# Layer A's product of probabilities with v of pairs 0 to 4 placed inside the next pair's key projection, ahead of its evacuation

## The chip, the core and the metric

The kernel runs on one core of one Trainium2 chip. The metric is the time of one execution on the device in microseconds (us). A core has a matrix engine (TensorE, PE in the profile, with its weight loads as PEld), a vector engine (VectorE, DVE), a scalar engine (ScalarE, ACT), a general engine (GpSimd, POOL) and an engine that here only starts transfers (SyncE, SP). Each works through its own list of instructions in order. Matmuls write to PSUM, of which this kernel holds four banks for projections (`ps_acc`) and four for everything else (`ps_side`).

## The reference, cut to what matters

Two layers over 512 tokens of width 1024, with 16 heads of 64. Layer A (the one that is touched) is attention in three dilation groups, merged by their denominators; layer B is attention over a two-dimensional neighbourhood. Each layer takes an RMS norm, one input projection (q, k, v of all groups and a gate), the mixer, a product with the gate, one output projection and a residual sum.

```python
def mixer_a(hn, w_in, w_out, q_gain, k_gain, t5_bias):
    proj = hn @ w_in
    qkv = proj[..., :n_qkv].reshape(b, s, N_DIL_GROUPS, 3, N_HEADS, HEAD_DIM)
    gate = proj[..., n_qkv:]
    for g, (window, dilation) in enumerate(DILATED_PAIRS):   # (128, 1), (512, 4), (2048, 16)
        q = rms_norm(qkv[:, :, g, 0], q_gain[g])
        k = rms_norm(qkv[:, :, g, 1], k_gain[g])
        v = qkv[:, :, g, 2]
        o, lse = dilated_group_attention(q, k, v, ...)       # softmax(q k * scale + bias) v
...
    alpha = jax.nn.softmax(jnp.stack(lses), axis=0)
    y = jnp.sum(alpha[..., None] * jnp.stack(outs), axis=0)
    y = y.reshape(b, s, BRANCH_WIDTH).astype(hn.dtype) * jax.nn.silu(gate)
    return y @ w_out
```

## The kernel before

**Tiling.** The 16 heads are handled as eight pairs (`hc` 0 to 7), 128 columns of q, k and v in each dilation group. The projections keep float32 accuracy by splitting each operand into a high and a low part and adding three products (`mm3`, L232), so one step over 128 rows of the contraction is three matmuls of 512 columns for each 128x512 result.

**The main stream (`main_a`, L628).** For each pair it runs four projections on TensorE: the keys of groups 1 and 2 with their v (`rawk`, 8 k-steps of 4 tiles of 3 matmuls, 96 in all), the three queries and the key of group 0 (`rawq`, 96), v of group 0 (`v0_a`, 24) and the gate (`gate_a`, 24). The weights come by DMA (`wraw`, L191) and are split into high and low part on ScalarE (L127) and on VectorE or GpSimd (L133), with four buffers of each. At the last k-step of `rawk` and `rawq` each of the four accumulators is evacuated by ScalarE (L530); then follow squares on GpSimd (L308), sums on VectorE (L311), the inverse root and the scaling (L330).

**The side stream (`side`, L1289).** One pair later, attention is worked in between the projections. For a pair p it runs, in this order:

- `move_q` (L684): the queries and keys, transposed on VectorE (L566), are written to a scratch buffer in DRAM (qd, L691) and read back (qt, L697) with rows and columns exchanged; `land` (L704) scales them on ScalarE (L758) once the next pair's key projection is stamped.
- `attn_a` (L886), in two halves u: scores (the tiles named log), softmax on VectorE (L929, L940) and ScalarE (L951, L802), and the transposing of the probabilities on VectorE (L865). `turner.send` (L867) writes them to a scratch buffer in DRAM (td, L874) and sets four reads back to come due (pt, L878).
- `weigh` (L962): the product of the probabilities with v, 52 small matmuls into two banks named o. `whole` (L778) adds the two banks (ScalarE copy L781, VectorE sum L782), and `put_y` (L804) multiplies by the gate (L822) and splits the result for the output projection (ScalarE L827, GpSimd L828). `attn_a` doesn't run this itself: it appends it to the list `pending`, from which a later point of the side stream takes it.

**What sets the order.** TensorE runs in the order in which the program is written down (`manual_schedule`, L55). That order is made by a planner, `run` (L1032): `clock[0]` adds up a cost for each matmul (512 columns by 1/2.4 ns, 213 ns, for those of the projections; L222), and after every three matmuls of the main stream `pump` (L1036) looks whether the side stream is due. A side step that yields a number is due that many ns later; one that yields nothing, 1200 ns later in layer A; one that yields `"wait", key, delay` is due `delay` ns after the planner's clock at which `key` was stamped:

```python
                if wait[0] is not None:
                    key, delay = wait[0]
                    if key not in stamp:
                        assert until is None, (key, until)
                        return
                    due[0] = max(due[0], stamp[key] + delay)
                    wait[0] = None
                if until is None and clock[0] < due[0]:
                    return
```

`stamp["rawk", hc]` is set when the key projection of pair hc is written down (`normed`, L556), `stamp["gate", hc]` when its gate projection is (`gated`, L785). `later_on` (L246) sets a job, most of them DMAs, to a planner's time, and `tick` (L251) runs what has come due. The order on the other engines comes from a scheduler, except that an instruction marked `keep_in_program_order` stays behind the one written before it on its engine. The writes of qd and td and the reads of qt and pt, all on SyncE, are marked so; the weight loads of layer A are not.

**The period.** With R as the planner's time of `stamp["rawk", hc]`, in planner-us: the weighing of pair hc - 2 is written down at R + 1.92 and costs 2.88; scores u = 0 of pair hc - 1 are due at R + 5.2 and u = 1 at R + 16.8 (12.5 for pair 0), each at a cost of 1.60; the probabilities of u = 1 are sent to td 9.0 after these scores, and their four reads come due 6.0, 6.5, 7.0 and 7.5 after the sending. `move_q` of pair hc is due 8.0 after the end of its query projection, the write of qd 0.6 later and the reads of qt 6.5 later. The gate of pair hc follows, and then the key projection of pair hc + 1.

Of the kernel before, what the change touches and what calls it, by code (L numbers as in the profile page):

```python
# [51 lines left out]
def tile_hybrid_encoder(  # L52
# [193 lines left out]
    def later_on(delay, job):  # L246

        timers.append((clock[0] + delay, job))
        timers.sort(key=lambda t: t[0])
# [494 lines left out]
    def v_a(hc):  # L744

        if hc < NHC - 1:
            return
        yield "wait", ("vt", hc), 2500
        vt = st.pop(("vt", hc))
        tp = bank("tp")  # L750
        for i in range(4):
            transpose(tp[:, i * P : (i + 1) * P], vt[:, i * P : (i + 1) * P])
        nc.scalar.copy(v0[hc % 2], tp.rearrange("p (i c) -> p i c", i=4))
        stamp["v", hc] = 0
        yield
# [48 lines left out]
    def put_y(hc, o, permuted, last):  # L804

        gt, rest = st.pop(("gate", hc))
        for _ in rest:
            pass
        if last and permuted:
            for c in range(4):  # L810
                q = slice(P * c, P * c + P)
                of = lambda t: t.rearrange("p (r c) -> p r c", r=8)[:, :, 16 * c : 16 * c + 16]
                nc.vector.tensor_mul(of(gt), of(gt), of(o))
                src = gt.rearrange("p (t a c) -> p c a t", t=4, a=2)[:, 16 * c : 16 * c + 16]
                h, l = (t[:, hc, q].rearrange("p (c a t) -> p c a t", c=16, a=2) for t in (st["y_h"], st["y_l"]))
                nc.scalar.copy(h, src)
                nc.vector.tensor_sub(l, src, h.bitcast(F32))
            return
        h, l, src = st["y_h"][:, hc, :], st["y_l"][:, hc, :], gt
        if permuted:  # L820

            tc.keep_in_program_order(nc.vector.tensor_mul(gt, gt, o))  # L822
            src = gt.rearrange("p (t a c) -> p c a t", t=4, a=2)
            h, l = (t.rearrange("p (c a t) -> p c a t", t=4, a=2) for t in (h, l))
        else:
            nc.vector.tensor_mul(gt, gt, o)
        nc.scalar.copy(h, src)  # L827
        (nc.vector if last else nc.gpsimd).tensor_sub(l, src, h.bitcast(F32))  # L828
        stamp["ya" if permuted else "yb", hc, "y"] = 0
# [56 lines left out]
    def attn_a(hc):  # L886
# [7 lines left out]
        def scores(u):  # L894

            tiles = []
            for t in (2 * u, 2 * u + 1):
                cs, n = (64, 192) if t == 0 else (0, 192) if t == 3 else (0, 256)
                tiles.append((t, [bank("log") for _ in range(2)], cs, n))
            for t, lgs, cs, n in tiles:  # L900
                ks = slice(P * t + cs, P * t + cs + n)
                parts = [(0, j, slice(cs, cs + n), k0[:, ks]) for j in range(4)] + [
                    (1 + g, j, slice(256 + P * g, 384 + P * g), qt[:, :, 4 + g, 32 * j : 32 * j + 32])
                    for g in range(2)
                    for j in range(4)
                ]
                for g, j, cols, keys in parts:
                    for hd in range(2):
                        hs = slice(64 * hd, 64 * hd + 64)
                        matmul(  # L910
                            lgs[hd][32 * j : 32 * j + 32, cols],
                            qt[hs, t, g, 32 * j : 32 * j + 32],
                            keys[hs],
                            share=2,
                            start=(g == 0),
                            stop=(g == 2),
                        )
            return [
                (hd, t, softmax(hd, t, lgs[hd], cs, n)) for t, lgs, cs, n in tiles for hd in range(2)
            ]  # L920
# [34 lines left out]
        def turn_p(hd, t, pr):  # L955
            tp = bank("tp")
            for i in range(4):
                transpose(tp[:, i * P : (i + 1) * P], pr[:, i * P : (i + 1) * P])
            dst = sb(pts[0], at(t, 0, hd, 0), [[128, 2], [32, 2], [512, 4], [1, 32]])
            nc.vector.tensor_copy(dst, tp.rearrange("p (g i a r) -> p g i a r", g=2, i=2, a=4))  # L960
# [31 lines left out]
        if hc < NHC - 1:  # L992
            for u in range(2):
                if moved(hc):
                    if pending and u == 0:
                        pending.pop(0)()
                        yield
                    yield "wait", ("rawk", hc + 1), 5200 if u == 0 else 16800 if hc else 12500
                else:
                    yield 6500 if u == 0 else 7000  # L1000
                turned = turner(512)
                turners.append(turned)
                for hd, t, pr in scores(u):
                    turned.put(pr, 512, 256 * hd + 64 * (t % 2), 128)
                send = partial(turned.send, pq[:, 2048 * u : 2048 * u + 2048], *((6000, 500) if u else (8500, 1200)))
                later_on(7000 + 2000 * u, send)
                if pending and u == 0:
                    yield 5000
                    pending.pop(0)()
            pending.append(lambda: put_y(hc, weigh(), True, False))  # L1010
        else:
            for u in range(2):
                if u == 0:
                    yield "wait", ("gate", hc), 500
                yield 600
                held = scores(u)
                yield 3200
                if pending:
                    yield "wait", ("gate", hc - 1), 16800
                    pending.pop(0)()  # L1020
                    yield
                for args in held:
                    turn_p(*args)
                    yield
            yield from v_a(hc)
            stamp["ya", "turned"] = 0
            put_y(hc, weigh(), True, True)
            yield

    pending = []  # L1030
# [258 lines left out]
    def side():  # L1289
        for k in range(KT):  # L1290
            norm(0, k, x_all[:, k, :])
            if k:
                square_a(k - 1)
            stamp["na", k] = 0
            if k == 4:
                gains()
            yield 1000
        square_a(KT - 1)
        for k in range(1, KT):
            yield 1300  # L1300
            nc.vector.tensor_add(x_all[:, 0, :], x_all[:, 0, :], x_all[:, k, :])
        yield 1500
        row_scale(row_sums(x_all[:, 0, :]))
        y = big.tile([P, 2 * KT * S], F32R, tag="y", name="y").rearrange("p (n k t) -> p n k t", n=2, k=KT)
        st["y_h"], st["y_l"] = y[:, 0], y[:, 1]
        yield 2500
        bias_lines()
        later_on(21000, lambda: st.__setitem__(("e", 0), bias_a(0)))
        yield 2500
        scales_a()  # L1310
        first_out()
        stamp["rs", "a"] = 0
        for hc in range(NHC):
            if hc < NHC - 1:
                yield from k_a(hc)
                yield from chain(q_a(hc), v_a(hc))
                if moved(hc):
                    yield from st.pop(("land", hc))
                yield from attn_a(hc)
                if hc == 1:  # L1320
                    bias_rows()
            else:
                gap[0] = cycle((500, 500, 700))
                yield from chain(q_a(hc), k_a(hc))
                yield from attn_a(hc)
        yield from residual(xg, 0)
        yield from residual(xg, 4)
        stamp["ya", KT - 1, "y"] = 0
        yield "wait", ("x", KT - 1), 800
        for f in range(KT):  # L1330
            square_b(f)
            yield 600
        yield 4500
        row_scale(row_sums(st.pop("ssq")))
        stamp["rs", "b"] = 0
        yield 5000
        nc.scalar.mul(rs_half, spread(), 0.5)
        stamp["rs", "all"] = 0
        for job, hc, delay in B_PLAN:
            yield "wait", ("b", "start"), delay  # L1340
            if job == "scores":
                yield from side_b(hc)
                continue
            yield "wait", ("back", hc), 3500
            if hc == NHC - 2:
                stamp["yb", "turned"] = 0
            pending.pop(0)()
            yield
            if hc >= NHC - 2:
                yield from residual(xm_d, 4 * (hc % 2))  # L1350

    run(main(), side())


# [98 lines left out]
```

## Time and profile before

| | us |
|---|---|
| median of 3 runs | 815.9 (813.92 to 817.93) |
| the profiled execution, its own time | 817.6 |
| its span, first to last instruction | 815.8 |
| mean granted clock of TensorE, share of full speed | 1.000 |
| VectorE busy | 532.0 |
| ScalarE busy | 434.6 |
| GpSimd busy | 246.9 |

The engines work at the same time, so busy times are not added. Layer A's eight pairs fill the first 540 us or so of the span; its output projection and layer B follow. In the rows below, a line such as L226 is the line of the kernel at which an instruction is issued (all matmuls pass through one helper, so they are told apart by the tile that they write: acc for projections, log for scores, o for the weighing, tp for transposes). "out<-in" names the tile that is written and those read; SPq is SyncE's queue of transfers, and "to landing" is the time from the issue of a DMA until its data are there.

### The profile page before, as it was taken

To read this page: it belongs to the slowest core of one execution; us is meant where nothing else is said; L and a number is where in the kernel's file an instruction comes from. 1 tells how busy PE (TensorE), PEld (TensorE's weight loads), DVE (VectorE), ACT (ScalarE), POOL (GpSimd) and SP (SyncE) were. 2 spreads that over 40 slices of the span, in tenths; PEclk is the share of its full clock that TensorE was granted. 3 is DMA by queue.
4 is the path that set the end of the run, shared out by engine and by line. 5 is a ranking of instruction groups with operands and counts; after the bars stand their busy time and mean duration, and the time that the engine had idled before them with its cause. 6 is when DMAs were issued, how large, how long until landed. Compare 5 with 4: busy or idle time off the path is not lost.

```text
span 815.8 us, 16172 instructions
## 1 busy us (share of the span) xinstructions
PE 808.5 (99%) x5972; PEld 662.2 (81%) x5972; DVE 532.0 (65%) x1364; ACT 434.6 (53%) x913; POOL 246.9 (30%) x400
## 2 busy tenths in 40 slices
PE   9999999999999999999999999999999999999998
PEld 7888888788888888888788888888888887778787
DVE  7466575665576576477476765538656989897824
ACT  7352752752752752662662564536337665757821
POOL 2262441542441441441432342111221315040100
PEclk9999999999999999999999999999999999999999
DMA  7367879779879779968858555157353887698664
GB/s 261 106 207 232 224 216 266 208 200 301 210 210 316 195 220 292 240 186 277 226 164 233 179 160 135 41 193 250 119 164 129 245 230 213 200 268 244 174 213 155
DMA packets 86478, 169.33 MB, mean 208 GB/s; under 512 B 7504, under 2 KB 45520, under 8 KB 86400
## 3 DMA queue, kind: packets, MB, share of 16 engines
q1 hardware_dynamic: 86256, 168.04, 70.0%
q8 instruction: 47, 0.77, 0.4%
q10 hardware_dynamic: 144, 0.26, 0.1%
q14 instruction: 31, 0.25, 0.1%
HBM read 126.21 MB, written 48.22 MB: 214 GB/s over the span
## 4 chain that ended last, share of the span: by engine, by line
PE 92%; DVE 3%; ACT 3%; DMA 1%; issue 1%; SPq 0%; DVEq 0%
PE acc L226 82%; PE log L226 5%; PE o L226 4%; ACT p L1222 1%; PE tp L230 1%; ACT p L1228 1%; DVE wl L133 1%; DMA eb<-eb_d 1%; DMA x_all<-in_xt 0%; DVE rawq L330 0%; DVE rawq L716 0%; PE pa L226 0%; DVE tr L865 0%; ACT wh L127 0%; PE pk L226 0%
## 5 line engine op out<-in xcount | busy, mean ns | idle before, releaser
L226 PE MATMUL acc<-wh,hn_h 128*128 128x512 f32 x704 | 278.8, 397 | 1.2 <-ACT hn_h L419 0.8
L226 PE MATMUL acc<-wl,hn_h 128*128 128x512 f32 x704 | 274.4, 391 | 0.0
L226 PE MATMUL acc<-wh,hn_l 128*128 128x512 f32 x704 | 274.3, 390 | 0.0
L127 ACT CAST wh<-wraw 128x512 fp32r<-128x512 f32 (+1 forms) x240 | 146.2, 613 | 227.0 <-PE acc L226 204.1
L133 DVE TENSOR_TENSOR wl<-wraw,wh 128x512 fp32r<-128x512 f32 (+1 forms) x169 | 121.7, 721 | 132.8 <-ACT wh L127 131.7
L133 POOL TENSOR_TENSOR wl<-wraw,wh 128x512 fp32r<-128x512 f32 (+1 forms) x72 | 94.3, 1310 | 237.8 <-ACT wh L127 228.4
L226 PEld LDWEIGHTS acc<-wh,hn_h 128*128 128x128 f32 x704 | 132.6, 189 | 32.9 <-issue 3.3
L226 PEld LDWEIGHTS acc<-wh,hn_l 128*128 128x128 f32 x704 | 132.7, 189 | 28.0
L226 PEld LDWEIGHTS acc<-wl,hn_h 128*128 128x128 f32 x704 | 132.8, 189 | 26.3
L308 POOL TENSOR_TENSOR sq<-rawq 128x256 f32<-128x256 f32 (+1 forms) x80 | 63.4, 806 | 87.1 <-ACT rawq L530 76.3
L226 PE MATMUL acc<-y,wh 128*128 128x512 f32 (+1 forms) x272 | 81.5, 383 | 0.0
L226 PE MATMUL acc<-hn_h,wh 128*128 128x512 f32 x192 | 75.5, 393 | 0.0
L226 PE MATMUL acc<-hn_l,wh 128*128 128x512 f32 x192 | 74.7, 389 | 0.0
L226 PE MATMUL acc<-hn_h,wl 128*128 128x512 f32 x192 | 74.7, 389 | 0.0
L865 DVE STREAM_TRANSPOSE tr<-p 128x512 f32<-128x512 f32 (+1 forms) x88 | 58.2, 677 | 19.8 <-ACT p L1228 9.0
L311 DVE TENSOR_REDUCE ss<-sq 128x4 f32<-128x256 f32 (+1 forms) x96 | 48.3, 505 | 34.3 <-POOL sq L308 27.4
L951 ACT ACTIVATE p<-p,mn 128x512 f32<-128x512 f32 (+1 forms) x64 | 44.9, 702 | 25.5 <-DVE mn L940 25.5
L226 PEld LDWEIGHTS acc<-y,wh 128*128 128x128 f32 x272 | 48.8, 188 | 9.4 <-issue 0.9
L330 DVE TENSOR_TENSOR rawq<-rawq,rs 128x256 f32<-128x256 f32 (+1 forms) x96 | 51.2, 593 | 5.3 <-POOL rs L119 4.9
L226 PE MATMUL acc<-y,wl 128*128 128x512 f32 (+1 forms) x136 | 51.3, 377 | 0.0
L530 ACT ACTIVATE rawq<-acc,rs_n 128x512 f32<-128x512 f32 (+1 forms) x76 | 44.2, 611 | 0.7 <-PE acc L226 0.2
L802 ACT ACTIVATE p<-p,mn 128x512 f32<-128x512 f32 (+1 forms) x64 | 43.4, 699 | 0.8 <-DVE mn L801 0.7
(142 smaller groups left out, 950.2 us busy)
## 6 DMA issues: line engine op xcount, KB each, us to landing
wraw<-in_w SPq DMA_DIRECT2D x111, 512.0 KB, 5.3
td<-tr SPq DMA_DIRECT2D x14, 1024.0 KB, 6.2
pt<-td SPq DMA_DIRECT2D x56, 256.0 KB, 6.4
qd<-rawq SPq DMA_DIRECT2D x6, 1536.0 KB, 6.6
qt<-qd SPq DMA_DIRECT2D x24, 384.0 KB, 7.4
td<-tr SPq DMA_DIRECT2D x8, 896.0 KB, 4.8
pt<-td SPq DMA_DIRECT2D x32, 224.0 KB, 6.5
v0x<-in_w SPq DMA_DIRECT2D x8, 512.0 KB, 6.0
```

Of the source, the lines that this page charges most:

```text
L127: nc.scalar.copy(h, raw)
L133: eng.tensor_sub(l, raw, h.bitcast(F32))
L226: nc.tensor.matmul(o, l, r, **kw)
L230: nc.tensor.transpose(o, i, ident)
L308: nc.gpsimd.tensor_mul(sq.rearrange("p (f a r) -> p a f r", a=4, r=32), v, v)
L311: nc.vector.tensor_reduce(ss[:, i * ns : (i + 1) * ns], sq.rearrange("p (a b) -> p a b", b=64), axis=AX.X, op=ALU.add)
L330: m = nc.vector.tensor_mul(v, v, by)
L530: nc.scalar.activation(dst, src, AF.Copy, scale=rs_n[:, i : i + 1])
L802: nc.scalar.activation(pr, pr, AF.Copy, scale=mn[:, 3:4])
L865: nc.vector.transpose(dst, src[:, :n].rearrange(order, b=4, k=32, **({"g": 2} if apart else {})))
L951: nc.scalar.activation(row, row, AF.Exp, bias=mn[:, 1:2], scale=-1.0, accum_out=mn[:, 2:3])
L1222: nc.scalar.activation(pr[:, o : o + n], pr[:, o : o + n], AF.Exp, bias=mn[:, 0:1], scale=-1.0, accum_out=mn[:, 2:3])
```

## The change

The weighing of pair hc - 1 is no longer taken from `pending` at the head of `attn_a(hc)`, which runs after the key projection of pair hc + 1 is stamped, but ahead of `land`, 9.0 planner-us after the gate of pair hc is stamped, while that key projection is being written down. `moved(hc)` holds for pairs 0 to 5, and `pending` is empty for pair 0, so the weighings of pairs 0 to 4 are concerned. Those of pairs 5 to 7 stay where they are. What the weighing computes is the same.

```diff
@@ -992,9 +992,6 @@
         if hc < NHC - 1:
             for u in range(2):
                 if moved(hc):
-                    if pending and u == 0:
-                        pending.pop(0)()
-                        yield
                     yield "wait", ("rawk", hc + 1), 5200 if u == 0 else 16800 if hc else 12500
                 else:
                     yield 6500 if u == 0 else 7000
@@ -1315,6 +1312,10 @@
                 yield from k_a(hc)
                 yield from chain(q_a(hc), v_a(hc))
                 if moved(hc):
+                    if pending:
+                        yield "wait", ("gate", hc), 9000
+                        pending.pop(0)()
+                        yield
                     yield from st.pop(("land", hc))
                 yield from attn_a(hc)
                 if hc == 1:
```

## The prediction

> **What bounds the kernel now.** I read the page first, then the table of waits for TensorE, then the chain of waits in order of time, and last SyncE's timeline for the transfers that the moved product needs.
>
> ```profile
> span 815.8 us, 16172 instructions
> PE 808.5 (99%) x5972; PEld 662.2 (81%) x5972; DVE 532.0 (65%) x1364; ACT 434.6 (53%) x913; POOL 246.9 (30%) x400
> ```
>
> TensorE is busy 808.5 of 815.8 us and runs its instructions in the order written. No matmul is added or removed, so the change can act only through the time in which TensorE stands still.
>
> ```profile
> PE log L226 <- issue: 1.8, 2, 1.1
> ```
>
> That row, from the waits, is all the standing still that layer A's attention has: two waits of the score matmuls (log), 1.8 us together, never more than 1.1. The chain shows where they are, and how the weighing (o) lies between the projections (acc). Columns: start, us, what, and matmuls with some of their weight loads counted in.
>
> ```profile
> 102.28 44.46 PE acc L226 x195
> 146.75 3.11 PE o L226 x104
> 149.85 1.59 PE acc L226 x6
> 151.44 1.53 PE log L226 x68
> 152.98 0.78 issue
> 153.76 0.66 PE log L226 x28
> 154.41 10.43 PE acc L226 x45
> 164.84 1.92 PE log L226 x90
> 166.76 43.06 PE acc L226 x189
> 209.82 3.11 PE o L226 x104
> ...
> 226.88 1.96 PE log L226 x90
> ...
> 288.89 1.93 PE log L226 x90
> ...
> 338.58 2.29 PE log L226 x82
> ...
> 351.30 1.92 PE log L226 x87
> ...
> 400.98 1.57 PE log L226 x75
> 402.55 1.05 issue
> 403.61 0.63 PE log L226 x21
> ```
>
> Each o block is one of the five that move. It follows 9 matmuls after a key projection's end: 6 more follow it, then comes the first half of the next pair's scores, then 45, then the second half (164.84). From there to the next o are 189 matmuls in 43.06 us, 0.228 us each: 36 left of the query projection, 24 of v, 24 of the gate, 96 of the next key projection, and 9. So o starts on the instant that its order gives; nothing of it is waited for.
>
> **Step 1: where the weighing goes.** It becomes due 9.0 planner-us after the stamp of the gate. The planner counts 0.2133 for a matmul and looks every three of them: 15 times 0.64 is the first sum that reaches 9.0, so 45 matmuls of the key projection stand ahead and 51 behind. Counted from the second half of the scores: these are due 16.8 planner-us after the key stamp, and the weighing (2.88 planner-us) no longer lies in that stretch, so 72 and not 60 matmuls precede them, and 24 of the query projection are left. Then come 24 of v, 24 of the gate and 45: 117 matmuls by 0.228 is 26.7 us, and with the scores' own 1.92 the weighing is reached 28.6 us after their start. For pair 0 the stretch ahead is old, and 195 less 60 matmuls give 102.28 + 30.8 = 133.1.
>
> **Step 2: what it needs by then.** All rows of the turned probabilities (pt), whose last quarter comes by DMA from a scratch buffer (td) through SyncE's one queue. SyncE's timeline, last column the count:
>
> ```profile
> 123.00 0.43 SPq L878 DMA_DIRECT2D pt<-td  x1
> ...
> 187.44 1.27 SPq L878 DMA_DIRECT2D pt<-td  x3
> 192.77 0.38 SPq L691 DMA_DIRECT2D qd<-rawq  x1
> 193.21 0.50 SPq L878 DMA_DIRECT2D pt<-td  x1
> ...
> 254.62 0.50 SPq L878 DMA_DIRECT2D pt<-td  x1
> ...
> 316.61 1.56 SPq L878 DMA_DIRECT2D pt<-td  x2
> ...
> 379.04 1.56 SPq L878 DMA_DIRECT2D pt<-td  x2
> ```
>
> The DMA view of the moments of these last issues (pairs 0, 1, 2, 3) gives the median time to landing; pair 4's row is the same as pair 3's:
>
> ```profile
> pt<-td SPq DMA_DIRECT2D x1, 256.0 KB, 10.3
> pt<-td SPq DMA_DIRECT2D x1, 256.0 KB, 7.5
> pt<-td SPq DMA_DIRECT2D x1, 256.0 KB, 7.9
> pt<-td SPq DMA_DIRECT2D x2, 256.0 KB, 7.7
> ```
>
> Landings are therefore 133.3 (pair 0), 200.7, 262.5, 324.3 and 386.7; for pairs 1 to 4 that is 35.9, 35.6, 35.4 and 35.4 us after the start of their second scores (164.84, 226.88, 288.89, 351.30), on average 35.6. Before, o comes 45 us after that start and has 9 us to spare. At 28.6 it is 7.0 us early. For pair 0 it is 0.2 early (133.1 against 133.3).
>
> **Step 3: how the landing itself moves.** The last read stands in the queue behind the write of the turned queries (qd), and this waits for VectorE's transposes of rawq, at the end of a chain that starts with the query projection's evacuation:
>
> ```profile
> 171.50 1.32 ACT L802 ACTIVATE p<-p,mn 128x512 f32<-128x512 f32 x2
> 173.76 2.40 ACT L530 ACTIVATE rawq<-acc,rs_n 128x512 f32<-128x512 f32 x4
> 190.38 2.36 DVE L566 STREAM_TRANSPOSE rawq<-rawq 128x1024 f32<-128x1024 f32 x2
> ```
>
> By the change the query projection ends 12 matmuls, 2.7 us, sooner after the scores. If the whole chain follows, qd leaves 2.7 us sooner and the wait is 4.3. But ScalarE works on the scores' softmax until 172.8, 8.0 us after their start, and only then evacuates; if that stays first, nothing is gained. On the other side, the planner's due times now fall the other way round: qd's write is due at 32.6 planner-us after the key stamp, the four reads at 34.2 to 35.7, where before three of them (two, for pairs 3 and 4) came due ahead of qd. All four reads, pinned in program order, now stand behind it: 0 to 0.9 us later (two more issues of 0.43). So the wait is 4.3 to 7.9 per pair; I take the middle of the shift and most of the issues, **6.3 us**. While o waits, the 51 matmuls and the key evacuation behind it wait too, and everything that they feed; nothing hides it, since TensorE is the bound. It returns at pairs 1 to 4: each period's chain is tied to its own key projection, so a wait doesn't spare the next one. 4 times 6.3 is 25.2, and pair 0's 0.2 makes 25.4.
>
> **Step 4: what goes, and what is free.** The two waits of 0.78 and 1.05 us in the scores come right behind a weighing: I take 1.8 off. All of the excess over a plain block of 1.92 us (2.97, 3.25 and 2.29 at 151.44, 400.98 and 338.58) would be 2.8; nothing would be 0.
>
> ```profile
> q8 instruction: 47, 0.77, 0.4%
> ```
>
> I read these 47 transfers as the supply of TensorE's instructions (5972 matmuls and as many weight loads); o and log are its densest stretches, so late instructions are my reading of the two waits. [...]
>
> The product's followers move with it. The copy and the sum are short, and go where ScalarE waits for TensorE 2 us ahead of each weight cast:
>
> ```profile
> L781 ACT COPY ow<-o x8: 566/587/588, 149.9 to 537.1; 128x512 f32<-128x512 f32 x8
> L782 DVE TENSOR_TENSOR ow<-ow,o x8: 679/687/689, 150.5 to 537.7; 128x512 f32<-128x512 f32 x8
> 202.38 0.62 ACT L127 CAST wh<-wraw 128x512 fp32r<-128x512 f32 x1 [2.05 <-PE acc L226]
> ```
>
> I cost them at nothing: the split weights are held four deep (four k-steps of 12 matmuls, 2.7 us each). If that cover were gone, they would cost their 1.3 us per pair. They carry no DMA. The weighing itself takes 3.11 us in either place.
>
> **The sum.** 25.4 less 1.8 is +23.6 us on the profiled execution, 817.6 us (span 815.8 and 1.8 around it). The median of the three runs, 815.9, is 1.7 lower: **839.5 us**, slower by 2.9%. Its own range: 4 times 4.3 less 2.8 is +14.4 (830), 4 times 7.9 with nothing saved is +31.6 (848).
>
> **Rivals.**
> *The data are there in time* (not slower). If the last read lands within 28.6 us of the scores' start, only the saving is left: 815.9 less 1.8, 814.1. For it: o never waits before. Against: all four landings are 7 us too late, and even the whole shift leaves 4.3. It decides at a landing 7.0 us sooner. Chance 0.12, of which 0.03 over 0.5% faster.
> *The reads go ahead of qd.* Then they leave as the first three of pair 1 did, at 187.44, 22.6 us after the scores; the DMA view of these three, with no qd ahead of them:
>
> ```profile
> pt<-td SPq DMA_DIRECT2D x3, 256.0 KB, 4.8
> ```
>
> Four issues take 1.7 and the landing 4.8; that is 29.1: 0.5 us of wait a pair, less 1.8, 816.1. Against: the order is pinned. Chance 0.06.
> *The clock falls after each wait.* TensorE has not stood still over 1.1 us in these stages, and the window from 396.30 that has a 1.05 us wait was granted 1.00:
>
> ```profile
> 396.30:456.00 59.70, 58.65 (x591) 48.24 (x599) 35.84 (x93) 32.78 (x59) 21.62 (x33) 1.00 0.66 194
> ```
>
> So a six-microsecond wait is unknown ground. Bounds: nothing, or the whole rest of the key projection at half pace (51 by 0.228, 11.6 us a pair). I count one k-step at half pace, nearer to the row: 2.7 a pair, 10.9 in all, 850.4. Chance 0.18. [...]
> *The accumulators come late instead.* v's projection needs a bank of the query projection, now wanted 7.4 us after the scores' start (1.92 and 24 matmuls), while the softmax holds ScalarE for 8.0 and one of the four evacuations (2.40) takes 0.6. At worst 1.2 us at five places, 6.0. In pairs 1 to 4 it lies inside the wait for pt; alone it would give 815.9 + 6.0 - 1.8 = 820.1. Chance 0.04.
>
> **How the numbers follow.** Forecast 0.60, clock 0.18, accumulators 0.04, data in time 0.12, reads ahead 0.06. About 0.5% (4 us) is what a measurement can tell from no change. Slower: 0.60 + 0.18 + 0.04 = 0.82; within: 0.09 + 0.06 = 0.15; faster: 0.03. The range must hold forecast, clock and some of the rest: 822 to 856.
>
> **What would show it.** Right: at pairs 1 to 4 the chain shows TensorE standing ahead of o for 4 to 8 us with a DMA (pt) as releaser, qd ahead of all four reads in SyncE's timeline, about 117 matmuls between the second scores and o, and no wait in the scores behind. Wrong: o starting without a wait (step 2), a wait of over 9 or under 3 us (step 3), reads ahead of qd, matmuls slower than 0.228 us behind the wait (the clock), or a wait ahead of v's projection.

## The result, and the profile after

| | before | after |
|---|---|---|
| median, runs on one chip | 815.16 us (4 runs) | 860.31 us (4 runs, 857.43 to 861.54) |
| ratio, 95% interval | | 1.0544 (1.0503 to 1.0585) |
| the profiled execution, its own time | 817.6 us | 859.13 us |
| its span | 815.8 us | 857.3 us |
| mean granted clock of TensorE | 1.00 | 0.98 |

The change makes the kernel slower by 5.4%. The forecast of 839.5 us had the sign and the wait that it named; it left out the slow clock behind that wait, and the time lies outside its range, which ended at 856. The engines' row of the page of after:

```profile
PE 818.7 (95%) x5972; PEld 670.1 (78%) x5972; DVE 537.3 (63%) x1364; ACT 435.3 (51%) x913; POOL 248.0 (29%) x400
```

The matmuls are the same 5972, yet TensorE is busy 10.2 us longer (808.5 before) and stands still for 38.6 us where it stood for 7.3. Together that is the 41.5 us by which the span has grown. Where it stands, from the waits of TensorE (us in total, times, longest), after and then the one row of before that the prediction didn't show:

```profile
PE o L226 <- issue: 21.1, 4, 7.3
PE o L226 <- DMA pt<-td: 8.4, 4, 6.6
PE acc L226 <- ACT rawq L530: 4.4, 5, 1.9
```

```profile
PE acc L226 <- ACT rawq L530: 0.4, 1, 0.4
```

The weighing (o) waits 29.5 us in pairs 1 to 4, 7.4 a pair, in two pieces: its first four matmuls wait for the third of four reads of pt, the others for the fourth. At pair 1 the first piece is put down to "issue", but the third read left at 194.78 and landed 8.2 us later, at 203.0:

```profile
203.09 0.69 PE L226 MATMUL o<-pt,rawk 64*64 64x128 f32 x4 [7.34 <-issue]
```

The chain of after shows what ended the second, the steps at pair 1 and the last ones of later pairs:

```profile
131.62 3.11 PE o L226 x104
...
164.35 5.09 DMA rp<-in_rpb
...
173.74 0.59 ACT rawq L530
...
192.75 0.38 SPq L691
...
193.73 1.00 SPq L878
...
194.78 1.23 SPq L878
196.05 8.25 DMA pt<-td
...
204.44 5.06 PE o L226 x98
...
268.98 8.08 DMA pt<-td
...
277.19 4.54 PE o L226 x98
...
349.36 5.97 PE o L226 x98
```

Read it from the end: the weighing at 204.44 waited for a read of pt, that for SyncE's issues (L878), and these for the write of qd (L691). Pair 0 (131.62) runs as before, without a wait, in 3.11 us. The others take 4.5 to 6.0 us for what is left of it once the last data are there (pair 4's 5.0 isn't shown). Windows of after at pair 1 say why (start and end, length, then busy time and count of PE, PEld, DVE, ACT, POOL, the granted clock, DMA share, GB/s):

```profile
194.71:198.12 3.41, 1.04 (x5) 0.54 (x3) 0.43 (x1) 0.00 (x0) 0.00 (x0) 1.00 1.03 320
198.00:199.00 1.00, 0.00 (x0) 0.00 (x0) 0.00 (x0) 0.00 (x0) 0.00 (x0) 0.56 0.92 245
204.95:208.36 3.41, 3.41 (x70) 3.41 (x67) 0.00 (x0) 0.00 (x0) 0.00 (x0) 0.50 1.09 305
208.00:209.00 1.00, 1.00 (x29) 1.00 (x25) 0.00 (x0) 0.00 (x0) 0.00 (x0) 0.82 1.13 237
204.44:277.19 72.75, 64.90 (x536) 53.21 (x537) 40.04 (x99) 33.47 (x64) 23.26 (x35) 0.95 0.73 209
```

While TensorE stands at pair 1, its granted clock goes from 1.00 to 0.50 (the slice from 198, 0.56 in the mean, holds the step), and it is still at 0.50 when the weighing begins (the stretch from 204.95). It comes back at 208.4, most of the way through it. The last row is one whole period, from the weighing of pair 1 to that of pair 2: 72.75 us with 64.90 busy. In before the same weighings stand 62.1 us apart, and all of it is busy. The sum between the two profiled executions: 29.5 for o, 4.0 more for the accumulators, 10.2 of slower work, less the 1.8 us of score waits that are gone, is 41.9 of the 41.5.

### The profile page after: what moved, and what is told of

The parts are those of the page before. It is cut to its first block, busy times and chain, and to the rows that moved or that the text cites. A ratio compares the mean times of both kernels' runs of the same rounds, so it can differ in the third digit from the quotient of the medians.

```text
span 857.3 us, 16170 instructions
## 1 busy us (share of the span) xinstructions
PE 818.7 (95%) x5972; PEld 670.1 (78%) x5972; DVE 537.3 (63%) x1364; ACT 435.3 (51%) x913; POOL 248.0 (29%) x400
## 4 chain that ended last, share of the span: by engine, by line
PE 76%; DVE 9%; DMA 6%; ACT 5%; issue 2%; SPq 1%; POOL 0%; DVEq 0%; ACTq 0%
PE acc L226 66%; PE o L226 5%; PE log L226 4%; DMA pt<-td 4%; DVE rawq L330 1%; DVE wl L133 1%; ACT p L951 1%; PE tp L230 1%; SPq L878 1%; ACT rawq L530 1%; DVE rawq L566 1%; ACT p L1219 1%; DVE rs L115 1%; DMA e<-l_d 1%; DMA rp<-in_rpb 1%
## 5 line engine op out<-in xcount | busy, mean ns | idle before, releaser
L133 DVE TENSOR_TENSOR wl<-wraw,wh 128x512 fp32r<-128x512 f32 (+1 forms) x169 | 128.6, 763 | 126.2 <-ACT wh L127 125.9
L133 POOL TENSOR_TENSOR wl<-wraw,wh 128x512 fp32r<-128x512 f32 (+1 forms) x72 | 96.2, 1336 | 301.9 <-ACT wh L127 288.1
L226 PE MATMUL o<-pt,rawk 64*64 64x128 f32 (+2 forms) x704 | 39.1, 331 | 29.4 <-issue 21.1
L951 ACT ACTIVATE p<-p,mn 128x512 f32<-128x512 f32 (+1 forms) x64 | 44.9, 702 | 35.7 <-DVE mn L940 34.6
L226 PEld LDWEIGHTS o<-pt,rawk 64*64 64x64 f32 (+1 forms) x704 | 31.1, 166 | 39.0 <-issue 35.3
```

Of the source, the lines that this page charges most:

```text
L133: eng.tensor_sub(l, raw, h.bitcast(F32))
L226: nc.tensor.matmul(o, l, r, **kw)
L951: nc.scalar.activation(row, row, AF.Exp, bias=mn[:, 1:2], scale=-1.0, accum_out=mn[:, 2:3])
```

## The experiments

**Reads first.** The write of qd comes due 3.4 planner-us later, so that the four reads of pt pass it. Nothing else differs from after.

```diff
-        later_on(600, write)
+        later_on(4000, write)
```

> The changed kernel, with the write of qd due 4.0 instead of 0.6 planner-us after the queries' transposes, so that all four reads of pt stand ahead of it in SyncE's queue; the weighing stays at its new place. Theory (the reads are late because they stand behind the qd write): the reads leave when td has landed, land about 30 us after the second scores, TensorE waits at most 2 us per pair, the weighing takes its 3.1 us again at full clock, and the accumulators cost their 4 us: 822 us (817 to 829). Rival A (the place is too early for the td round trip whatever the queue's order): the wait stays over 5 us per pair, 845 or more. Rival B (the weighing is slow at this place for another reason than the clock): it still takes about 5 us, 830.

Measured: 819.93 us beside 815.79, ratio 1.0047 (1.0031 to 1.0062). SyncE's timeline of this run at pair 1, then the same stretch of after, with the write at the next pair:

```profile
190.53 1.74 SPq L878 DMA_DIRECT2D pt<-td  x4
193.09 0.38 SPq L691 DMA_DIRECT2D qd<-rawq  x1
```

```profile
192.75 0.38 SPq L691 DMA_DIRECT2D qd<-rawq  x1
193.22 3.91 SPq L878 DMA_DIRECT2D pt<-td  x4
...
265.66 0.38 SPq L691 DMA_DIRECT2D qd<-rawq  x1
```

The DMA views of the two stretches give the landing of these reads (KB, median us from issue), first in this run, then in after with the write ahead:

```profile
pt<-td SPq DMA_DIRECT2D x4, 256.0 KB, 4.1
```

```profile
qd<-rawq SPq DMA_DIRECT2D x1, 1536.0 KB, 6.6
pt<-td SPq DMA_DIRECT2D x4, 256.0 KB, 8.2
```

Without the write ahead, four issues take 1.74 us and land 4.1 later; behind it, 3.91 and 8.2. The waits of TensorE in this run:

```profile
PE acc L226 <- ACT rawq L530: 4.0, 6, 1.2
```

In this run one order in one queue is therefore worth 40 of the 45 us. The granted clock is 1.00 and the weighing takes 3.11 to 3.17 us at the new place, so the slow clock went with the waits. What stays is mostly the accumulators' wait, 3.6 us more than before, against the 1.8 us saved.

**The wait filled.** 34 matmuls of 512 columns stand ahead of the weighing, into banks that it then starts afresh, so that TensorE works where it would wait. First for all five pairs, then for pairs 1 to 4 only (`34 if 0 < hc < 5 else 0`).

```diff
         def weigh():
...
             o = [bank("o") for _ in range(2)]
+            for n in range(34 if hc < 5 else 0):
+                nc.tensor.matmul(o[n % 2], wide(P), wide(S), start=True, stop=True)
```

> The changed kernel, with 34 matmuls of 512 columns on constant data ahead of each of the five moved weighings, written to its own two banks, which the weighing then overwrites; they only keep TensorE busy for some 7.3 us. Theory (the clock falls while TensorE waits, and that makes the weighing behind it slow): in pairs 1 to 4 they fill the wait, the granted clock stays at 1.00, the weighing takes 3.1 us instead of 5, and the time falls by 8 to 10 us, less about 7 for pair 0, which has no wait to fill: 857 at no fall of pair 0's cost, range 853 to 859, with the windows of pairs 1 to 4 each 2 to 2.5 us shorter than in the changed kernel. Rival B (the weighing is slow for another reason, such as the supply of instructions or traffic): it stays at 5 us, and the time rises by pair 0's 7 us to 867.

> The run with 34 filling matmuls ahead of the moved weighings, without those of pair 0, which had no wait to fill. Theory (the clock falls while TensorE stands still): TensorE is kept from work for as long as in the changed kernel, but at full clock, so the weighing takes 3.1 to 3.6 us and the time is the changed kernel's 860 less 8 to 10: 851 us (849 to 854). Rival (the weighing is slow for another reason): 858 to 862.

Measured: 860.21 us, ratio 1.0548 (1.0525 to 1.057), and 854.5, ratio 1.0479 (1.0459 to 1.0498). Both are a little above their expected ranges. The second run's page, its group of filling matmuls, and its chain at pair 1:

```profile
PE 838.7 (98%) x6108; PEld 686.8 (81%) x6108; DVE 536.6 (63%) x1364; ACT 435.4 (51%) x913; POOL 249.1 (29%) x400
```

```profile
L966 PE MATMUL o<-ones 128*128 128x512 f32 x136 | 30.4, 381 | 0.0
```

```profile
203.82 3.17 PE o L226 x98
```

Take the filling away from the busy time: 838.7 - 30.4 is 808.3, what before has (808.5). All 10.2 us of slower work are gone, the weighing takes 3.17 us, and the clock is 1.00 throughout, though its data land just as late (203.82 against 204.44). So here the slow clock came with standing still and went when the wait was filled, and it is a cost beside the wait. That the time falls by only 5.8 us fits: the filling is 7.6 us a pair where 7.4 were waited, and 3.4 us of waits for pt are left, so 4.3 us go back. The first run also fills pair 0, which has no wait to fill, and is 5.7 us slower than the second.

**Later in the keys.** The weighing half way further towards the end of the key projection, and nearly at its end:

```diff
-                        yield "wait", ("gate", hc), 9000
+                        yield "wait", ("gate", hc), 14000
```

(18500 in the other run.)

> The changed kernel, with the weighing due 14.0 instead of 9.0 planner-us after the gate, 21 matmuls (4.8 us) later. Theory: the wait falls by just that, from 7.4 to 2.6 us per pair; if the clock falls only in a wait of some length (over 3 us), the weighing is back at 3.1 us: 815.2 + 4 x 2.6 + 4 - 1.8 = 828 us (824 to 832). If the loss by the clock is in proportion to the wait, 4 us more, 832. Rival (the wait is not set by a landing at a fixed time): the wait doesn't fall by 4.8, and the time stays over 840.

> The changed kernel, with the weighing due 18.5 instead of 9.0 planner-us after the gate: still inside the key projection and ahead of its evacuation, but 42 matmuls (9.6 us) later. Theory: the landing is then 2 us before the weighing; no wait, full clock, the weighing takes 3.1 us; what stays is the accumulators' wait ahead of v's projection (4 us), less the score waits (1.8): 817 us (814 to 820). Rival A gives the same here. Rival B (slow at any place inside the key projection): 2 us at five places more, 825 to 828.

Measured: 838.64 us, ratio 1.0277 (1.0252 to 1.0301), and 826.79, ratio 1.0141 (1.0115 to 1.0166). Both expectations missed by 10 us. The waits for pt did what the landing times said. Half way:

```profile
PE o L226 <- issue: 9.1, 5, 2.7
...
PE o L226 <- DMA pt<-td: 2.4, 3, 0.9
```

That is 2.9 us a pair, and at 18500 no wait for pt is left; instead the accumulators wait there, up to 3.0 us:

```profile
PE acc L226 <- ACT rawq L530: 8.4, 6, 3.0
```

Two things had been left out. Shorter waits were followed by the slow clock too (2.7 to 3.4 us at o in pairs 1, 3 and 4 half way; 3.0, 2.1 and 2.1 us for the accumulators in the later run): TensorE is busy 817.1 us in the half-way run, 8.6 more than before, and 811.5 in the later one, 3.0 more. 12.9 and 10.2 us of this work fall into stretches at 0.50. There the later run's projections start a matmul every 0.43 us (175.76 to 178.32), and every 0.23 us at 1.00 (from 179.00), so half pace, taken as exactly half, costs some 6.5 and 5.1, an estimate; the rest of the 8.6 isn't explained. And at 18500 the accumulators' wait is 8.4 us where 4 was expected; why it grew wasn't tested. The later run's time falls into the range of its rival B, but not for that reason: its weighings are as fast as before (o is busy 39.5 us in both). Windows of the later one, at pair 1 and pair 3, and then of the half-way one, at pair 1 and pair 2:

```profile
175.00:176.00 1.00, 1.00 (x4) 0.81 (x4) 0.58 (x2) 1.00 (x3) 0.93 (x2) 0.69 0.00 0
301.67:305.09 3.42, 1.47 (x6) 1.23 (x7) 2.48 (x6) 3.42 (x8) 1.53 (x3) 1.00 0.44 110
305.00:306.00 1.00, 1.00 (x5) 0.74 (x4) 0.66 (x2) 1.00 (x3) 1.00 (x2) 0.54 0.00 0
308.00:309.00 1.00, 1.00 (x5) 0.74 (x5) 0.84 (x1) 0.13 (x1) 1.00 (x2) 0.75 0.00 0
```

```profile
205.00:211.00 6.00, 5.52 (x96) 5.55 (x98) 0.00 (x0) 0.00 (x0) 0.00 (x0) 0.50 1.04 243
269.33:272.75 3.42, 1.98 (x9) 1.31 (x7) 0.69 (x1) 0.62 (x1) 0.00 (x0) 1.00 1.06 230
272.75:276.16 3.41, 2.23 (x69) 2.04 (x73) 0.00 (x0) 0.00 (x0) 0.00 (x0) 1.00 1.06 295
```

In the stretch from 301.67 a wait of 2.1 us was enough: TensorE was at work again before 305 and was slowed only then (0.54 in the slice from 305). In the half-way run pair 1 weighed at half clock, while pair 2, with 2.6 us of waiting in two pieces spread over two stretches, kept 1.00.

**Is it the weighing's place that makes the accumulators late?** The weighing stays where it was before; only the second half of the scores comes 2.9 planner-us later, as near to the end of the query projection as the change brings it.

```diff
-  yield "wait", ("rawk", hc + 1), 5200 if u == 0 else 16800 if hc else 12500
+  yield "wait", ("rawk", hc + 1), 5200 if u == 0 else 19700 if hc else 12500
```

> The kernel before, weighing at its old place, with only the second scores of pairs 1 to 5 due 19.7 instead of 16.8 planner-us after the key stamp, so that the end of the query projection is as close behind them as in the changed kernel (and all four reads of pt again stand behind the write of qd). Theory (the wait for the accumulators ahead of v's projection comes from this distance alone, since the softmax keeps ScalarE): waits of 0.7 to 2 us at four or five places, with half clock behind those near 2 us, 820 us (818 to 824), and no wait at the weighing, which has some 4 us to spare. Rival (the wait comes from the weighing's own followers at the new place): no such waits, 815 to 816.

Measured: 827.9 us, ratio 1.0149 (1.0127 to 1.017).

```profile
PE acc L226 <- ACT rawq L530: 3.9, 6, 0.8
PE acc L226 <- ACT rawk L530: 2.2, 2, 1.4
```

The wait for rawq is there, with the weighing where it was: the scores' nearness to the end of the query projection is enough to make it. The time is 8 us above the number expected and 4 above its range; 2.2 of it are a second wait, for rawk, and TensorE is also 3.1 us longer busy (811.6). Of that, 2.7 lie in the scores themselves (log is busy 48.9 us, 46.2 in before); why they run slower at a clock of 1.00 stays open.

**Then scores sooner should take it away.** Three runs set the second scores earlier: by 2.9 planner-us with the weighing at 18500, by 2.9 with the reads first, and by 1.2 with the reads first.

```diff
-  ... 5200 if u == 0 else 16800 if hc else 12500
+  ... 5200 if u == 0 else 13900 if hc else 12500
```

(15600 in the last.)

> The changed kernel with the weighing due 18.5 planner-us after the gate (as in the run with the late place) and the second scores due 13.9 instead of 16.8 after the key stamp, so that their distance to the query projection's end is that of the kernel before. Theory: neither the landing nor the accumulators are waited for, the clock stays, and the two waits in the scores (1.8 us) are gone: 813.5 us (812 to 815.5). Rival (the place inside the key projection costs something by itself, as the late place's 826.8 may suggest): over 818.

> The changed kernel with the weighing at its new place (9.0 planner-us after the gate), the write of qd due 4.0 instead of 0.6 after the queries' transposes, and the second scores due 13.9 instead of 16.8. Theory: both causes are taken away where the change put the weighing; no wait, full clock: 813.5 us (812 to 816). Rival (this place costs by itself): 818 or more.

> The changed kernel with the four reads of pt ahead of the write of qd in SyncE's queue, and with the second scores two groups of the query projection sooner (due time 15600 in place of 16800). Theory: what is left of the change with the reads first (4.0 us, 1.2 in pair 1 and 0.7 in each later pair) is the softmax of the second scores, still on ScalarE when the query projection ends, so that its evacuation comes late; scores that start about 1.4 us sooner take the 0.7 us away in pairs 2 to 4 and leave some 0.5 to 1.2 in pair 1, where GpSimd still waits for a transfer: no wait for pt, the clock at 1.00 and about 817 us (815 to 819). Rival: any sooner place meets VectorE's work on the key projection of the pair before, as 3900 sooner did (2900 in the due time), so the softmax ends no sooner and the accumulators' waits stay: 820 to 822 us.

Measured: 825.95 us, ratio 1.0129 (1.011 to 1.0148); 821.8, ratio 1.009 (1.0061 to 1.0119); 820.49, ratio 1.0055 (1.0042 to 1.0069). The theory missed three times, by 12, 8 and 3.5 us. The last run's wait, its VectorE timeline and its ScalarE timeline at pair 2:

```profile
PE acc L226 <- ACT rawq L530: 6.1, 5, 1.5
```

```profile
228.99 1.30 DVE L566 STREAM_TRANSPOSE rawq<-rawq 128x512 f32<-128x512 f32 x2
...
230.79 0.41 DVE L929 CUSTOM_DVE_ANT_0 p<-log,e 128x256 f32<-128x256 f32 x1
```

```profile
232.00 0.73 ACT L951 ACTIVATE p<-p,mn 128x512 f32<-128x512 f32 x1 [3.96 <-DVE mn L940]
...
237.73 0.72 ACT L802 ACTIVATE p<-p,mn 128x512 f32<-128x512 f32 x1
238.36 2.39 ACT L530 ACTIVATE rawq<-acc,rs_n 128x512 f32<-128x512 f32 x4
```

and VectorE's turning and first softmax step in the run with the reads first alone:

```profile
229.27 1.30 DVE L566 STREAM_TRANSPOSE rawq<-rawq 128x512 f32<-128x512 f32 x2
...
231.46 0.42 DVE L929 CUSTOM_DVE_ANT_0 p<-log,e 128x256 f32<-128x256 f32 x1 [0.33 <-PE log L226]
```

There VectorE waited 0.33 us for the scores. With the scores sooner it doesn't wait; it is still turning the projected rows (L566) and starts the softmax 1.80 us after that step's start instead of 2.19, so only 0.4 us earlier. ScalarE waits 3.96 us for that, and then its list has the last softmax step (237.73) ahead of all four evacuations. This is what the last run's rival said, 820 to 822 us included. The rivals of the other two runs (818 or more) had the numbers too; the cost of the place that they name shows there as the accumulators' wait, 7.7 and 6.0 us. With the reads first, neither of the two sooner times did better than 16800 (819.93), and the accumulators' wait rose from 4.0 to 6.0 and 6.1; other places weren't tried. No version beat before.

## Why the prediction was right in kind and wrong in size

**Step 1, the place: held.** At pair 1 TensorE stops ahead of o at 195.75 (1.04 us busy in the stretch from 194.71), 30.9 us after its second scores, which start at 164.8 as before. Predicted were 28.6; the accumulators' 1.9 is most of the difference. The count of 117 matmuls between them was right.

**Step 2, that the data come too late: held** for pairs 1 to 4. Pair 0's 0.2 us didn't show.

**Step 3, how the landing moves: the order held, one term was mis-sized.** All four reads stand behind qd at every pair. Pair 2's second scores in TensorE's timeline of after:

```profile
239.60 0.66 PE L226 MATMUL log<-k,qt 64*32 64x256 f32 x16
```

Half of the shift came too: qd leaves 26.06 us later (at 265.66), in before 27.3 (254.20 less 226.88), so 1.3 of 2.7; at pair 1 there was none: GpSimd waited for a transfer (rp, in the chain), and the softmax ahead of the evacuation for GpSimd. But the extra issues, put at "0 to 0.9 us later" ("two more issues of 0.43"), cost about 3. By the prediction's own rows it is three more at pairs 1 and 2; each took up to 1.23 us behind the 1.5 MB write and not 0.43; and the last landed 8.1 to 8.25 us after its issue, where 7.5 to 7.9 had been read. The data came 37.5 us after pair 2's scores (277.06 less 239.6) where 28.6 + 6.3 = 34.9 was predicted. The wait at o grew less, to 7.4 a pair: the accumulators' wait ahead of it and the four first matmuls of o, which don't need the last quarter, took the rest. The term measured 29.5 for 25.4, and 33.5 with the accumulators' 4.0.

At pair 1 the reads landed a median 8.2 us after their issue behind the write (after) and 4.1 without it ahead (reads first); no run here tells the queue's order from the traffic of the write.

**Step 4: the saving held, the weighing's own time didn't.** The two waits in the scores are gone, 1.8 us. "The weighing itself takes 3.11 us in either place" is the sentence that failed: with its first four matmuls it took 5.2 to 6.6, and the term, put at nothing, was 10.2 us in all. The slow work lies in the weighings alone: o is busy 50.1 us where it was 39.5, the projections (acc) are within 0.3 of before, and the scores 1.1 shorter. TensorE was at work for 19.1 us of the stretches at 0.50; taken as exactly half pace, that costs half of it, 9.6, an estimate. The price had been worked out, as a rival, at 2.7 a pair and 10.9 together; it measured 2.6 and 10.2. That fits in the mean only: by pairs the half is 1.8 to 3.2, and one k-step at half pace was a choice between bounds. The half pace was the author's estimate: in before the mean granted clock is 1.00 and no half pace shows; after showed 0.50, for 6.8 to 10.2 us at each of the four pairs.

**The clock was no rival.** That is the larger fault behind the size. It had a chance of 0.18, as if it stood against the forecast, but the forecast's own six-microsecond waits were its condition. Forecast and clock together are 23.6 + 10.9 = 34.5, against 41.5 measured between the two profiled executions; the other 7 are step 3's term, 33.5 for 25.4, less small differences. The accumulators' wait was put inside the wait for pt, and at pair 2 that fits: VectorE takes up v's projection on the way to qd, at 253.72, but had been at work until 253.59, so without that wait qd would have left some 0.1 us sooner, and TensorE would have stood at o instead. No run takes that wait away by itself. The medians lie 45.2 apart: the profiled execution of before was 2.4 above its median, that of after 1.2 below.

Of the signs named ahead, the DMA as releaser, qd ahead of the reads, the slow matmuls and the wait ahead of v's projection were all seen. **The reads ahead of qd**, a rival at 816.1, measured 819.93 when that order was made; the accumulators' wait, which its price left out, is 3.6 us of the difference.

## What to carry to other kernels

Before moving a consumer earlier, follow its operand's DMA back through its queue: here the order of one write and four reads was worth 40.4 us, ten times the 4.1 that were left of the change without it. A wait on TensorE cost more than its length here where it left 1.47 us of work or less in one of the 3.41 us stretches between which the clock changed (and in two of four with 1.62 to 1.64), so price a predicted wait with the slow work behind it. Ask of each rival whether it excludes the forecast or comes with it, and add those that come with it and don't already lie inside one of its waits.

## What the runs showed of the hardware

**In four traces the clock changed on a grid of 3.413 us.** There, from 100 to 450 us, it was 1.00 or 0.50 on either side of a step, so a slice's mean tells when within it the step came. In after, 0.56 in the slice from 198 puts the fall at 198.12, and 0.82 in that from 208 puts the rise at 208.36: 10.24 us, three times 3.413. In the later-in-the-keys run the falls are at 175.38 and 305.08, 129.70 apart, 38 times 3.413, and the second rise is at 308.50, one step on. In the four (after, the two later places, and the later place with sooner scores) all 24 falls and rises, worked out so, are whole steps of 3.413 apart within their run, to 0.03 us.

**Stretches that were not idle were followed by half clock here.** That from 194.71 in after had TensorE busy for 1.04 of 3.41 us, that from 301.67 in the later-in-the-keys run for 1.47 of 3.42, and the next was at 0.50 each time; 1.98 kept the clock (269.33 half way). In these four traces, from 164 to 431 us, every stretch at 1.00 with 1.47 us of work or less was followed by 0.50, and every one with over 1.64 by 1.00. In between, in the run with the weighing at 18500 and sooner scores, four stretches were busy for 1.62 to 1.64 us; two of them kept the clock and two lost it. One of each, with the stretch behind it:

```profile
237.66:241.07 3.41, 1.63 (x8) 1.05 (x7) 2.66 (x4) 3.41 (x7) 1.62 (x3) 1.00 0.00 0
241.07:244.48 3.41, 3.41 (x16) 2.80 (x16) 1.85 (x4) 2.58 (x5) 3.41 (x4) 1.00 0.83 198
302.51:305.93 3.42, 1.62 (x7) 1.03 (x6) 2.22 (x4) 3.42 (x8) 2.42 (x3) 1.00 0.13 25
305.93:309.34 3.41, 3.41 (x9) 2.67 (x8) 2.06 (x3) 1.30 (x4) 3.41 (x5) 0.50 0.93 250
```

So in these traces a wait of some 2 us was or wasn't followed by 3.4 us at half pace, by where it fell on the grid; single waits of up to 1.7 us never were. How busy a stretch must be for the clock to come back isn't settled by these runs: in after 2.86 us of work at 0.50 were followed by 1.00 (276.63), and 2.87 by 0.50 (348.31).
